# State-out weights of the S5 layer: imaginary parts on VectorE beside the gates, 25 of 32 pieces there instead of 19

## The chip, the core and the metric

The kernel runs on one core of a Trainium2 chip. The metric is device microseconds of one launch; lower is better. Engine names below: PE is TensorE, DVE is VectorE, ACT is ScalarE, POOL is GpSimd, SP is SyncE, which here only issues DMAs.

## The reference, cut to what matters

Two residual layers over 512 latent and 256 context tokens of width 1024. Layer 0 is multi-head latent attention with 16 heads and a SiLU gate of width 2048. Layer 1 is a bidirectional S5 state-space layer: 128 channel groups, each with 64 complex states in each direction.

```python
q_dn, kv_dn, k_rope, gate = split(h @ w_in)        # layer 0: the gate is 2048 wide = 16 tiles of 128
y = (softmax(q k^T) v * silu(gate)) @ w_out

lam_bar = exp(lam * dt)                            # layer 1, per direction, complex
xs[t]   = lam_bar * xs[t-1] + b_bar * u[t]
y[t]    = real(sum over states of xs[t] * cmat)    # two directions are summed
```

The kernel takes 8 tokens at a time as a block, so it needs, for each group, the complex products of `cmat` with the powers 0 to 7 of `lam_bar`: the state-out weights. They don't depend on the tokens. They are made in 32 pieces of 4 groups each.

## The kernel before, in words

The program goes through stages in order of time: modulation and first projections (to about 104 us), the 16 gate tiles of layer 0 (to 305 us), attention (from 331 to 757 us), layer 0's output projection, and then layer 1 (from about 890 us to the end). While layer 0 runs, the weights of layer 1's state space are prepared beside it: first the parameters (`s5_params`, on DVE and POOL, until 133 us), then the 32 pieces of state-out weights (`s5_chunk`, lines 335 to 373), then 32 pieces of state-in weights (`win_load` to `win_early`, lines 379 to 409) on POOL.

A piece of `s5_chunk` does this. SP loads `cb` (L339, two buffers), the `cmat` and `bmat` of four groups. POOL makes the real part `wr = cr*pr - ci*pi` (L351 to L353) and the imaginary part `wi = cr*pi + ci*pr` (L354 to L356) in the tile `wo`, with the scratch `wt1` of one buffer, then `b1`, `b2` (L361, L363) and two additions into `bk` (L367). `bks` are two tiles in turn, so the additions of a piece wait for the PE products of the piece two before. What comes after a piece is put off by one piece (`late`): `s5_lags` (lines 313 to 333) stores `wo` on SP's queue to `wod`, lets PE multiply `bk` with `wo` (L320, L323; below these are the lag products), has ACT and DVE copy the result to `ks` (L326, L327), and stores it on SP's queue with eight DMAs to `kd` (L330, L331). After every fourth piece SP copies `kd` to `toed` with eight DMAs (L311, `s5_lay`).

19 pieces (`S5IN`) run in the gate stage and 13 in attention. In the gate stage `tables(n)` is called behind each gate tile `m`; it emits one piece, or two at `m` = 3, 7, 11 and 15, and none at `m` = 0. The gate loop's other work: `gate(m)` takes 48 matmuls (L81, L82, L83) with a weight tile that ACT and DVE have split (L65), `mod_more` loads a part of the second layer's modulation weights on ACT's queue into one of two buffers `pair` and multiplies it (L103), `s5_coefs` runs at `m` = 4 (L296, L299), and the first head's query preparation at `m` = 11 to 13. PSUM tiles of the stage come from one pool of six buffers (`mm`). In attention a piece is emitted at every 1.6th of 80 units (a head's quarter of queries each, and a fifth unit for context); from unit `LAST` on, `win_early` is called in two of three units.

Each engine runs its own instructions in order. The order between engines' instructions is written down once, by a scheduler that works before the launch, so the place of an instruction in its queue is fixed, and an instruction that waits holds up all behind it on its engine.

Of the kernel before, what the change touches and what calls it, by code (L numbers as in the profile page):

```python
# [13 lines left out]
ALU = mybir.AluOpType  # L14
# [17 lines left out]
def hybrid_mla_s5(ctx, tc, I, O):  # L32
# [5 lines left out]
    pe, dve, act, pool, sp = nc.tensor, nc.vector, nc.scalar, nc.gpsimd, nc.sync  # L38
# [107 lines left out]
    G, Gd = [], {}  # L146


    GR, NCH, S5IN, WO = 128, 32, 19, [3]
    lamd = dram.tile([P, 2, GR], F32, name="lamd")  # L150
    pind = dram.tile([8, GR, 2, P], F32, name="pind")
    wod = [dram.tile([P, 4, 2, P], F32, name=f"wod{i}") for i in range(NCH)]
# [138 lines left out]
    def s5_coefs(cps, mm, tile):  # L291

        for k, cp in enumerate(cps):
            o = mm(256).rearrange("p (r x) -> p r x", r=2)
            for r in range(2):
                pe.transpose(o[:, r, :], cp[:, r, :], ident)  # L296
            st = tile()[:, :2 * P].rearrange("p (r x) -> p r x", r=2)
            act.copy(st[:, 0, :], o[:, 0, :])
            act.mul(st[:, 1, :], o[:, 1, :], -1.0)  # L299
            act.dma_start(out=pind[7 - k, :, :, 0:64], in_=st[:, :, 0:64])  # L300
            act.dma_start(out=pind[k, :, :, 64:128], in_=st[:, :, 64:128])
# [3 lines left out]
    def s5_lay():  # L305

        while whole:
            k = whole.pop()
            src = kd[k].rearrange("g c x -> c g x")
            for i in range(8):  # L310
                sp.dma_start(out=toed[k][16 * i:16 * i + 16], in_=src[:, :, 16 * (7 - i):16 * (7 - i) + P])  # L311

    def s5_lags(work, mm, c, wo, bk, dcol, eyek):

        sp.dma_start(out=wod[c], in_=wo)
        s5_lay()
        o = mm(P)
        for r in range(2):
            for q in range(4):
                pe.matmul(o[32 * q:32 * q + 32, :], bk[:, q, r, 0:32], wo[:, q, r, :], start=(r == 0), stop=False)  # L320
        for r in range(2):
            for q in range(4):
                pe.matmul(o[32 * q:32 * q + 32, 0:16], bk[:, q, r, 16:48], wo[:, q, r, 112:128],  # L323
                          start=False, stop=(r == 1))
        ks = work.tile([P, P], F32, name="ks", bufs=2)
        act.copy(ks[:, 16:P], o[:, 16:P])  # L326
        dve.scalar_tensor_tensor(ks[:, 0:16], eyek, dcol[:, c:c + 1], o[:, 0:16], op0=ALU.mult, op1=ALU.add)  # L327
        for q in range(4):
            g = 4 * (c % 4) + q
            sp.dma_start(out=kd[c // 4][g, :, 112:240], in_=ks[32 * q:32 * q + 16, :])  # L330
            sp.dma_start(out=kd[c // 4][g, :, 0:112], in_=ks[32 * q + 16:32 * q + 32, 0:112])  # L331
        if c % 4 == 3:
            whole.append(c // 4)

    def s5_chunk(work, mm, c, pw, cci, bks, dcol, eyek, end):

        def load(c):
            cbs[c] = work.tile([P, 4, 2, 32], F32, name="cb", bufs=2)
            sp.dma_start(out=cbs[c], in_=I["CB"][:, 4 * c:4 * c + 4])  # L339
        gs = slice(4 * c, 4 * c + 4)  # L340
        if c not in cbs:
            load(c)
        if c < end:
            load(c + 1)
        cb = cbs.pop(c)
        wo = work.tile([P, 4, 2, P], F32, name="wo", bufs=WO[0])
        t = work.tile([P, 4, 8, 16], F32, name="wt1", bufs=1)
        cr, ci = (cb[:, :, r, 0:16].unsqueeze(2).broadcast_to([P, 4, 8, 16]) for r in range(2))
        pr, pi = (pw[:, r, :, gs].rearrange("p j g -> p g j").unsqueeze(3).broadcast_to([P, 4, 8, 16]) for r in range(2))
        wr, wi = (wo[:, :, r, :].rearrange("p g (j c) -> p g j c", c=16) for r in range(2))  # L350
        pool.tensor_tensor(wr, cr, pr, op=ALU.mult)  # L351
        pool.tensor_tensor(t, ci, pi, op=ALU.mult)  # L352
        pool.tensor_tensor(wr, wr, t, op=ALU.subtract)  # L353
        pool.tensor_tensor(wi, cr, pi, op=ALU.mult)  # L354
        pool.tensor_tensor(t, ci, pr, op=ALU.mult)  # L355
        pool.tensor_tensor(wi, wi, t, op=ALU.add)  # L356

        b1 = work.tile([P, 4, 2, 16], F32, name="b1", bufs=1)
        b2 = work.tile([P, 4, 2, 16], F32, name="b2", bufs=1)
        bb = cb[:, :, :, 16:32]  # L360
        pool.tensor_tensor(b1, bb, cci[:, 0:2, gs].rearrange("p r g -> p g r").unsqueeze(3).broadcast_to([P, 4, 2, 16]),  # L361
                           op=ALU.mult)
        pool.tensor_tensor(b2, bb[:, :, ::-1, :], cci[:, 2, gs].unsqueeze(2).unsqueeze(3).broadcast_to([P, 4, 2, 16]),  # L363
                           op=ALU.mult)
        bk = bks[c % 2]
        for d, rows in enumerate((lo_, up_)):
            pool.tensor_tensor(bk[rows, :, :, 16 * d:16 * d + 16], b1[rows], b2[rows], op=ALU.add)  # L367
        late.append(lambda: s5_lags(work, mm, c, wo, bk, dcol, eyek))
        while len(late) > (c < end):
            late.pop(0)()  # L370
        if c == end:
            s5_lay()
# [38 lines left out]
    with ExitStack() as ctx_:  # L411
# [14 lines left out]
        def chunk(work, mm, c, end):  # L426
            s5_chunk(work, mm, c, pw, cci, bks, dcol, eyek, end)
# [103 lines left out]
        with mkpool(name="in_h", bufs=KC) as hp, mkpool(name="in_w", bufs=3) as wp, \  # L531
# [3 lines left out]
            def mm(n=512):  # L535
                return ps.tile([P, 512], F32, name="mm")[:, :n]
# [151 lines left out]
            def spill():  # L688
                while spills:
                    m = spills.pop()  # L690
                    Gd[m] = dram.tile([P, T], F32, name=f"gd0{m}")
                    act.dma_start(out=Gd[m], in_=G[m])

            def gate(m):
                w = wg.pop(0)
                G.append(gv.tile([P, T], F32, name="G") if m >= HEADS - KEPT else gsp.tile([P, T], F32, name="Gs"))
                gate_w()
                for a, b in LC:
                    o = mm(b - a)
                    proj_mm([o], w, range(KC), [(a, b)])  # L700
                    yield 1
                    act.activation(G[m][:, a:b], o, AF.Tanh, scale=0.5)
                    spill()
                    dve.scalar_tensor_tensor(G[m][:, a:b], G[m][:, a:b], 1.0, o, op0=ALU.add, op1=ALU.mult)
                if m < HEADS - KEPT:
                    spills.append(m)
# [40 lines left out]
            def mod_more():  # L747

                n = next(done)
                ends.get(n - 3, lambda: None)()  # L750
                if len(ready) == 2 or n > 24 and ready:
                    ready.pop(0)()
                for load, step in itertools.islice(steps, 1):
                    load()
                    ready.append(step)
            todo = iter(range(S5IN))

            def tables(n):
                for c in itertools.islice(todo, n):
                    chunk(s5in, mm, c, S5IN - 1)  # L760
            prep0 = dict(zip(range(11, HEADS), prep(0)))
            for m in range(HEADS):
                for _ in gate0 if m == 0 else gate(m):
                    mod_more()
                if m == 4:
                    s5_coefs(cps, mm, t512)
                for fn in prep0.pop(m, ()):
                    fn()
                tables((m > 0) + (m % 4 == 3))
            spill()  # L770
            sces.close()
        gv2 = gvs.enter_context(mkpool(name="gv2", bufs=HEADS - KEPT, side="right"))
# [226 lines left out]
    def res_load(tt, n):  # L999

        c = slice(512 * n, 512 * n + 512)
        if (n, tt // 4) not in gates0:
            g = gates0[n, tt // 4] = xp.tile([P, 512], F32, name="g", bufs=2)
            sp.dma_start(out=g, in_=gtrow[0][tt // 4:tt // 4 + 1, c].broadcast_to([P, 512]))
        x = xp.tile([P, 512], F32, name="x")
        sp.dma_start(out=x, in_=I["xp"][tt * P:(tt + 1) * P, c])
        return x, gates0[n, tt // 4]
# [4 lines left out]
    for h in range(HEADS):  # L1012
# [4 lines left out]
        if h < 9:  # L1017
            if 2 <= h < 8:
                tt = h - 2
                x, g = res_load(tt, 0)  # L1020
# [197 lines left out]
    for t in range(18):  # L1218
# [9 lines left out]
        m = t - 2  # L1228
# [90 lines left out]
    def glu_mm():  # L1319
        m, k, h = GLU_ORDER.pop(0)  # L1320
        wh, wl = wnext()
        if h == 0:
            if m % 4 in (1, 2):
                acc[m, k] = bank()
            elif k:
                t = two(m % 4 == 0)
                acc[m, 1], acc[m, 0] = t[:, 0], t[:, 1]
        for j in range(8):
            c = slice(j * P, (j + 1) * P)
            mm3(acc[m, k], wh[:, c], wl[:, c], *V[8 * h + j], (h, j) == (0, 0), (h, j) == (1, 7))  # L1330
        return m, k, h
# [33 lines left out]
    while GLU_ORDER:  # L1365
        m, k, h = glu_mm()
        if (k, h) == (0, 1):
            g = work.tile([P, TL], F32, name="g")
            sp.dma_start(out=g, in_=gd[m])
            t = work.tile([P, TL], F32, name="t2")  # L1370
# [10 lines left out]
    with mkpool(name="f_s", bufs=1, side="right") as work:  # L1381
# [34 lines left out]
        for tt in range(4):  # L1416
# [5 lines left out]
            for n in range(2):  # L1422
                c = slice(512 * n, 512 * n + 512)
# [106 lines left out]
```

## Time and profile before

| what | us |
|---|---|
| median of 3 runs | 1726.29 (1719.12 to 1726.81) |
| the profiled execution | 1721.6 |
| its span | 1719.5 |
| PE busy in the span | 1558.3 (91%) |
| DVE, ACT, POOL busy | 966.9, 728.7, 652.0 |
| POOL's last work in the attention stage | 749 |

PE is the engine with the most work, and from 757 us on it has little idle time. The stages in which other engines decide lie before that. Marks on the time line that are used below: the lag products of the first piece start at 136.15 us, gate tile 3 starts at 137 us, the last matmul of gate tile 15 starts at 304.93 us, and attention's first score matmul (L803) starts at 331.26 us.

### The profile page before, as it was taken

The page shows a single profiled execution, that of the slowest core. Times are in us where ns is not written, and L with a number is a line of the kernel's source. Part 1 is how long each engine was busy: PE and PEld are TensorE (multiplying, and loading weights), DVE is VectorE, ACT ScalarE, POOL GpSimd, SP SyncE. Part 2 cuts the span into 40 slices and gives each one's busy share as a digit, 9 for nine tenths or more (in the row PEclk, how much of TensorE's full clock was granted, in tenths as well). Part 3 has the DMA queues.
Part 4 walks back from the last instruction along what each step waited for, and adds up shares of the span by engine and source line. Part 5 has one row for each costly group of instructions (what it writes and reads, how often), then busy time and mean ns, then how long its engine had stood idle before and what let it go on. Part 6 is the DMA issues. An engine that isn't in the chain of part 4 may idle for free.

```text
span 1719.5 us, 26866 instructions
## 1 busy us (share of the span) xinstructions
PE 1558.3 (91%) x9870; PEld 1301.2 (76%) x9870; DVE 966.9 (56%) x2502; ACT 728.7 (42%) x1253; POOL 652.0 (38%) x682
## 2 busy tenths in 40 slices
PE   7867979499889999799999999999679999999997
PEld 4645857388778888688879999888568888888876
DVE  6541233177667887683372688899853333323347
ACT  2421222166446666563235666766562222222220
POOL 2999958859679989940021000000000000000022
PEclk9978999699999999999999999999889999999999
DMA  9266774443456666644327766398443333333432
GB/s 344 67 205 210 241 242 141 150 144 116 139 170 209 208 196 193 204 158 139 105 83 236 225 220 233 117 367 291 155 156 115 110 112 104 116 104 109 145 139 74
DMA packets 156459, 291.89 MB, mean 170 GB/s; under 512 B 55004, under 2 KB 86280, under 8 KB 155304
## 3 DMA queue, kind: packets, MB, share of 16 engines
q1 hardware_dynamic: 104112, 234.99, 40.0%
q10 hardware_dynamic: 52104, 55.03, 10.7%
q8 instruction: 78, 1.28, 0.3%
q14 instruction: 53, 0.43, 0.1%
q0 software_dynamic: 112, 0.16, 0.0%
HBM read 229.54 MB, written 68.70 MB: 173 GB/s over the span
## 4 chain that ended last, share of the span: by engine, by line
PE 59%; POOL 12%; DMA 10%; DVE 9%; ACT 4%; issue 3%; SPq 1%; ACTq 0%; POOLq 0%; DVEq 0%
PE mm L81 16%; PE mm L83 16%; PE mm L82 16%; PE mm L1157 3%; PE tr L842 2%; DMA wraw<-in_wout_dram 2%; DMA ext<-pind 2%; PE mm L1291 1%; DMA cb<-in_CB_dram 1%; POOL wo L356 1%; DMA toed<-kd 1%; POOL wo L354 1%; POOL wo L353 1%; POOL wt L355 1%; POOL wt L352 1%
## 5 line engine op out<-in xcount | busy, mean ns | idle before, releaser
L65 DVE TENSOR_TENSOR wlo<-wraw,whi 128x1024 fp32r<-128x1024 f32 (+1 forms) x155 | 179.1, 1157 | 327.7 <-ACT whi L65 324.4
L65 ACT CAST whi<-wraw 128x1024 fp32r<-128x1024 f32 (+1 forms) x155 | 149.3, 965 | 406.3 <-PE mm L82 270.9
L1394 POOL TENSOR_TENSOR x<-x,row_g 128x1024 f32<-128x1024 f32 x4 | 9.6, 2402 | 767.6 <-DMA x<-x1d 728.7
L81 PE MATMUL mm<-st,whi 128*128 128x512 f32 x512 | 204.1, 399 | 5.5 <-ACT st L76 5.4
L83 PE MATMUL mm<-st,wlo 128*128 128x512 f32 x512 | 202.7, 396 | 0.0
L82 PE MATMUL mm<-st,whi 128*128 128x512 f32 x512 | 201.2, 393 | 0.8 <-DVE st L77 0.8
L81 PE MATMUL mm<-h,whi 128*128 128x512 f32 (+1 forms) x384 | 139.4, 364 | 0.2 <-DVE bnmv L934 0.2
L82 PE MATMUL mm<-h,whi 128*128 128x512 f32 (+1 forms) x384 | 137.4, 358 | 0.6 <-DVE h L1094 0.6
L83 PE MATMUL mm<-h,wlo 128*128 128x512 f32 (+1 forms) x384 | 137.0, 357 | 0.0
L81 PEld LDWEIGHTS mm<-st,whi 128*128 128x128 f32 x512 | 97.5, 190 | 27.0 <-ACT st L76 6.6
L81 PE MATMUL mm<-hh,whi 128*128 128x512 f32 (+1 forms) x320 | 109.6, 355 | 7.3 <-ACT wmod L299 5.4
L82 PEld LDWEIGHTS mm<-st,whi 128*128 128x128 f32 x512 | 97.3, 190 | 23.4 <-DVE st L77 1.6
L83 PEld LDWEIGHTS mm<-st,wlo 128*128 128x128 f32 x512 | 97.3, 190 | 22.6
L83 PE MATMUL mm<-hh,wlo 128*128 128x512 f32 (+1 forms) x320 | 108.4, 343 | 1.8 <-DVE wlo L65 1.8
L82 PE MATMUL mm<-hl,whi 128*128 128x512 f32 (+1 forms) x320 | 109.4, 344 | 0.0
L818 ACT ACTIVATE p<-sc,mx 128x768 f32<-128x768 f32 (+1 forms) x96 | 73.5, 766 | 45.6 <-DVE mx L817 36.7
L65 DVE TENSOR_TENSOR ptl<-tr,pth 128x384 fp32r<-128x384 f32 (+1 forms) x160 | 78.7, 522 | 17.9 <-ACT pth L65 17.2
L65 ACT CAST pth<-tr 128x384 fp32r<-128x384 f32 (+1 forms) x160 | 68.1, 462 | 37.9 <-PE tr L842 31.6
L817 DVE TENSOR_REDUCE mx<-sc 128x1 f32<-128x768 f32 (+1 forms) x96 | 73.6, 770 | 18.4 <-PE sc L807 17.3
L81 PEld LDWEIGHTS mm<-h,whi 128*128 128x128 f32 x384 | 73.2, 191 | 12.1 <-issue 0.7
L82 PEld LDWEIGHTS mm<-h,whi 128*128 128x128 f32 x384 | 73.3, 191 | 11.0 <-DVE h L1094 1.1
L83 PEld LDWEIGHTS mm<-h,wlo 128*128 128x128 f32 x384 | 73.1, 191 | 10.4
(376 smaller groups left out, 4178.9 us busy)
## 6 DMA issues: line engine op xcount, KB each, us to landing
wraw<-in_wglu_dram SPq DMA_DIRECT2D x64, 512.0 KB
wraw<-in_win_dram SPq DMA_DIRECT2D x36, 512.0 KB
wod<-wo SPq DMA_DIRECT2D x32, 512.0 KB
pw<-in_Bc_dram SPq DMA_DIRECT2D x32, 512.0 KB
pt<-wid SPq DMA_DIRECT2D x32, 512.0 KB
wo<-wod SPq DMA_DIRECT2D x32, 512.0 KB
pair<-in_w_mod_dram ACTq DMA_DIRECT2D x16, 768.0 KB
wo<-pind SPq DMA_DIRECT2D x21, 512.0 KB
```

The lines of the kernel that those rows point to most:

```text
L65: return act.copy(hi, src).ins, (eng or dve).tensor_tensor(lo, src, f(hi), op=ALU.subtract).ins
L81: pe.matmul(ps, lh, rh, start=first, stop=False)
L82: pe.matmul(ps, lh, rl, start=False, stop=False)
L83: pe.matmul(ps, ll, rh, start=False, stop=last)
L352: pool.tensor_tensor(t, ci, pi, op=ALU.mult)
L353: pool.tensor_tensor(wr, wr, t, op=ALU.subtract)
L354: pool.tensor_tensor(wi, cr, pi, op=ALU.mult)
L355: pool.tensor_tensor(t, ci, pr, op=ALU.mult)
L817: dve.reduce_max(mx[:, 1:2], s, axis=AX.X, negate=True)
L818: act.activation(p[:, a:b], s, AF.Exp, bias=mx[:, 1:2], scale=1.0, accum_out=mx[:, 2:3])
L842: pe.transpose(tp[:, n, :], p[:, j * P:(j + 1) * P], ident)
L1157: pe.matmul(o[:, r, 96 * q:96 * (q + 1)], wi[:, q, r, :], us[m][:, 4 * (c % 2) + q, :], start=True, stop=True)
```

## The change

`S5IN` goes from 19 to 25, so 25 pieces are emitted beside the gates and 7 in attention; `LAST`, the attention unit from which `win_early` is called, goes with it from 20 to 11 by the line `LAST = 8 * (NCH - S5IN) // 5`. For the first 25 pieces the three operations of the imaginary part are issued on DVE instead of POOL, and their scratch is a PSUM tile of the gate stage's pool `mm` instead of `wt1`. `tables` emits two pieces behind each gate tile from `m` = 3 on, and none before.

```diff
-    GR, NCH, S5IN, WO = 128, 32, 19, [3]
+    GR, NCH, S5IN, WO = 128, 32, 25, [3]
...
         pool.tensor_tensor(wr, cr, pr, op=ALU.mult)
         pool.tensor_tensor(t, ci, pi, op=ALU.mult)
         pool.tensor_tensor(wr, wr, t, op=ALU.subtract)
-        pool.tensor_tensor(wi, cr, pi, op=ALU.mult)
-        pool.tensor_tensor(t, ci, pr, op=ALU.mult)
-        pool.tensor_tensor(wi, wi, t, op=ALU.add)
+
+        eng, t = (dve, mm(512).rearrange("p (g j c) -> p g j c", j=8, c=16)) if c < S5IN else (pool, t)
+        eng.tensor_tensor(wi, cr, pi, op=ALU.mult)
+        eng.tensor_tensor(t, ci, pr, op=ALU.mult)
+        eng.tensor_tensor(wi, wi, t, op=ALU.add)
...
-                tables((m > 0) + (m % 4 == 3))
+                tables(2 if m > 2 else 0)
```

Lines behind the edit move by two: L354 to L356 become L356 to L358, and L367 becomes L369.

On PE, in the queue of the kernel before, around the end of gate tile 2 (the last rows of it, then modulation products, then the lag products of the first piece, then gate tile 3, whose rows are again `hh`, 128x512):

```order
L81 MATMUL mm<-hh,whi 128x256
L82 MATMUL mm<-hl,whi 128x256
L83 MATMUL mm<-hh,wlo 128x256
L103 MATMUL modps<-pair,sT 2x384 x32
L320 MATMUL mm<-wo,ext 32x128 x8
L323 MATMUL mm<-wo,ext 32x16 x8
L81 MATMUL mm<-hh,whi 128x512
```

In the kernel after the change, gate tile 3 follows gate tile 2 directly; this is the end of its first half, the start of its second, with two modulation products inside:

```order
L83 MATMUL mm<-hh,wlo 128x512
L103 MATMUL modps<-pair,sT 2x384 x4
L81 MATMUL mm<-hh,whi 128x512
L82 MATMUL mm<-hl,whi 128x512
L83 MATMUL mm<-hh,wlo 128x512
L81 MATMUL mm<-hh,whi 128x256
L82 MATMUL mm<-hl,whi 128x256
L103 MATMUL modps<-pair,sT 2x384 x4
L83 MATMUL mm<-hh,wlo 128x256
```

and this its end, with three more modulation products (x12 is three times four), the first lag products, and gate tile 4:

```order
L82 MATMUL mm<-hl,whi 128x256
L83 MATMUL mm<-hh,wlo 128x256
L103 MATMUL modps<-pair,sT 2x384 x12
L320 MATMUL mm<-wo,ext 32x128 x8
L323 MATMUL mm<-wo,ext 32x16 x8
L81 MATMUL mm<-hh,whi 128x512
```

Gate tile 3 has moved ahead of the first lag products and of most of the modulation products that stood in front of it; three modulation products have moved behind the first lag products.

On DVE, in the kernel before, around one gate tile in the middle of the stage (`Gs` is a gate's last operation, `wlo` the split of a gate's weights, `ks` that of a lag product):

```order
L327 SCALAR_TENSOR_TENSOR ks<-eyek,dcol,mm 128x16
L704 SCALAR_TENSOR_TENSOR Gs<-Gs,mm 128x512
L65 TENSOR_TENSOR wlo<-wraw,whi 128x1024
L704 SCALAR_TENSOR_TENSOR Gs<-Gs,mm 128x256
L327 SCALAR_TENSOR_TENSOR ks<-eyek,dcol,mm 128x16
```

and in the kernel after the change:

```order
L65 TENSOR_TENSOR wlo<-wraw,whi 128x1024
L706 SCALAR_TENSOR_TENSOR Gs<-Gs,mm 128x256
L356 TENSOR_TENSOR wo<-cb,pw 128x4x128
L327 SCALAR_TENSOR_TENSOR ks<-eyek,dcol,mm 128x16
L924 TENSOR_TENSOR aff<-modc_1590,lnc 128x16
L925 TENSOR_TENSOR aff<-modc_1590,lnc 128x16
L327 SCALAR_TENSOR_TENSOR ks<-eyek,dcol,mm 128x16
L357 TENSOR_TENSOR mm<-cb,pw 128x512
L926 TENSOR_TENSOR aff<-aff,modc_1590 128x16
L358 TENSOR_TENSOR wo<-wo,mm 128x4x128
L356 TENSOR_TENSOR wo<-cb,pw 128x4x128
L357 TENSOR_TENSOR mm<-cb,pw 128x512
```

The operations of the imaginary part (L356 to L358) now stand between the gate's and the lag products' operations, and some `ks` stand behind an L356 of a later piece, which waits for that piece's `cb`.

## Rows read from the trace of the kernel before

**Rows 1.** Stages, 137 to 305 and 305 to 331 us: busy time, clock, DMA.

```profile
core 0: us, PE busy (x) PEld busy (x) DVE busy (x) ACT busy (x) POOL busy (x), PEclk, DMA share, GB/s
137.00:305.00 168.00, 147.91 (x1309) 119.76 (x1298) 48.88 (x92) 36.54 (x86) 140.57 (x160) 0.94 0.64 202
305.00:331.00 26.00, 3.52 (x98) 2.38 (x97) 1.70 (x5) 3.20 (x7) 25.60 (x31) 0.58 0.40 121
```

**Rows 2.** What PE waited for, 296 to 345 us: total, times, longest.

```profile
PE mm L320 <- POOL wo L356: 12.4, 2, 7.8
PE mm L320 <- POOL wo L353: 9.7, 1, 9.7
```

**Rows 3.** POOL by line, 113 to 337 us: busy us, mean ns, idle before.

```profile
L356 POOL TENSOR_TENSOR wo<-wo,wt 128x512 f32<-128x512 f32 x21 | 27.7, 1323 | 0.9
L353 POOL TENSOR_TENSOR wo<-wo,wt 128x512 f32<-128x512 f32 x21 | 27.7, 1317 | 0.6
L354 POOL TENSOR_TENSOR wo<-cb,pw 128x512 f32<-128x512 f32 x21 | 25.6, 1217 | 0.0
L352 POOL TENSOR_TENSOR wt<-cb,pw 128x512 f32<-128x512 f32 x22 | 24.3, 1105 | 0.9
L355 POOL TENSOR_TENSOR wt<-cb,pw 128x512 f32<-128x512 f32 x21 | 23.2, 1105 | 0.9
L351 POOL TENSOR_TENSOR wo<-cb,pw 128x512 f32<-128x512 f32 x21 | 23.2, 1105 | 23.2 <-DMA cb<-in_CB_dram 15.0 <-issue 7.9
L367 POOL TENSOR_TENSOR ext<-b,b 64x128 f32<-64x128 f32 x42 | 22.9, 545 | 1.6
L361 POOL TENSOR_TENSOR b<-cb,ext 128x128 f32<-128x128 f32 x21 | 10.9, 517 | 0.0
L363 POOL TENSOR_TENSOR b<-cb,ext 128x128 f32<-128x128 f32 x21 | 8.8, 420 | 0.0
```

**Rows 4.** What PE waited for, 104 to 137 us.

```profile
PE modps L103 <- DMA pair<-in_w_mod_dram: 17.8, 8, 5.0
```

**Rows 5.** POOL in order of time: start us, us; the first piece's additions.

```profile
135.11 0.98 POOL L367 TENSOR_TENSOR ext<-b,b 64x128 f32<-64x128 f32 x2
```

**Rows 6.** PE in order of time: the lag products ahead of gate tile 4.

```profile
147.41 0.65 PE L320 MATMUL mm<-wo,ext 128*32 128x128 f32 x16 [0.20 <-POOL ext L367]
```

**Rows 7.** SP's queue in order of time, 281 to 306 us.

```profile
281.54 0.42 SPq L331 DMA_DIRECT2D kd<-ks  x1
282.00 0.42 SPq L330 DMA_DIRECT2D kd<-ks  x1
...
282.98 0.37 SPq L339 DMA_DIRECT2D cb<-in_CB_dram  x1
283.46 0.37 SPq L315 DMA_DIRECT2D wod<-wo  x1
...
303.62 2.60 SPq L311 DMA_DIRECT2D toed<-kd  x4
```

**Rows 8.** What SP's queue waited for, 137 to 331 us.

```profile
SPq L339 <- POOL wt L355: 28.2, 7, 7.0
```

**Rows 9.** DVE by line and form, 137 to 331 us: busy us, mean ns.

```profile
L65 DVE TENSOR_TENSOR wlo<-wraw,whi 128x1024 fp32r<-128x1024 f32 x10 | 15.7, 1572 | 29.3 <-ACT whi L65 27.4 <-DMA wmod<-in_bgt_dram 1.8
```

**Rows 10.** The same view, 1300 to 1600 us, where POOL does nothing.

```profile
L65 DVE TENSOR_TENSOR wlo<-wraw,whi 128x1024 fp32r<-128x1024 f32 x55 | 67.4, 1226 | 170.8 <-ACT whi L65 169.9
```

**Rows 11.** Score matmuls of L803, two a unit: busy (count) in two stretches.

```profile
431.00:531.00 100.00, 12.72 (x36) 7.21 (x36) 0.95 0.54 165
545.00:643.00 98.00, 13.63 (x40) 7.53 (x40) 1.00 0.61 201
```

**Rows 12.** PE by line and form, 340 to 470 us, with 13 pieces.

```profile
L320 PE MATMUL mm<-wo,ext 128*32 128x128 f32 x208 | 8.7, 279 | 1.4 <-POOL wo L356 1.4
...
L323 PE MATMUL mm<-wo,ext 128*32 128x16 f32 x208 | 3.8, 182 | 0.0
```

**Rows 13.** What PE waited for, 530 to 740 us.

```profile
PE sc L803 <- ACT pair L65: 6.8, 2, 5.9
```

## The prediction, made before the changed kernel ran

> **What bounds the kernel now.** I read the busy time by stages first, then what PE waited for where it idles, then the engine it waited for, line by line, and last the queues. The change touches the gate stage and attention, so only what happens before 757 us can move. From 137 us, where gate tile 3 starts, to 305 us, where gate tile 15 ends, PE is busy for 147.9 of 168 us. Then it is nearly idle, 3.5 of 26 us, until attention's first score matmul at 331.3 us, and the granted clock is 0.58 there, while POOL is busy for 25.6 of these 26 us [rows 1]. PE waits there for lag products of the last pieces, whose `wo` POOL has not made: 12.4 and 9.7 us [rows 2]. So the stage ends by POOL. Its price per piece is the sum of means: L351 1.105, L352 1.105, L353 1.317, L354 1.217, L355 1.105, L356 1.323, L361 0.517, L363 0.420 and twice L367 at 0.545, together 9.20 us, and there are 23.2 us of idle time ahead of L351, 15.0 of them put down to `cb` [rows 3]. Nineteen pieces at 9.20 and the idle time make 198 us, which is what lies between the end of the parameters (133 us) and 331. SP in turn waits for POOL: 28.2 us before it may load the next `cb` [rows 8]. DVE has work for 48.9 of 168 us [rows 1], and DMA stands at a share of 0.64.
>
> **The imaginary part on DVE, what POOL loses.** L354, L355 and L356 leave POOL: 3.645 us a piece, so 5.55 us stay. What DVE pays for them no row shows for this shape, so from the nearest: a subtraction of twice as many elements, with both inputs in SBUF, takes 1226 ns while POOL does nothing [rows 10] and 1572 ns in the gate stage [rows 9]. So 0.61 us is the price of one in peace, and 0.35 us what POOL's company adds. The two products read two SBUF tiles, 0.96 each; the addition reads PSUM for one of its inputs, 0.61. That is 2.5 us a piece and 63 us for 25, beside DVE's 49 in a stage of some 170: DVE has the room. POOL pays for the company too: its mean for L354 is 0.11 over that of L351, the same shape [rows 3]. A product on DVE can hold it up for nothing at least and for the whole 0.61 at most, so 0 to 1.2 us a piece. I take 0.7, nearer to the upper end because DVE's own loss is more than half of a price in peace: 6.25 us a piece.
>
> The Trainium skill says more on this ("SBUF — State Buffer", section "Who interferes with whom"): a DVE instruction with two SBUF inputs contends with a GpSimd instruction that reads SBUF, and whoever comes second is blocked for the whole of the other. The 346 ns between [rows 9] and [rows 10] agree with it. By that rule POOL would pay at the upper end, 6.75 us a piece, and what this gives is the second rival below.
>
> **The head of the stage.** Before, PE waits 17.8 us in 104 to 137 us for eight loads of modulation weights [rows 4], and gate tile 3 stands behind all of them and behind the first lag products. Those need POOL's additions of piece 0, which start at 135.1 us [rows 5]. Gate tile 4 starts behind the lag products of 147.41 + 0.65 [rows 6], at 148 us. After, gate tile 3 stands ahead of most of these waits and three of the modulation products stand behind the lag products. The tile takes some 9 us, less than the 17.8 us of waits that it now fills. The additions come earlier by what stands ahead of them in POOL's order now, three L354, two L355 and two L356, 8.5 us by [rows 3], less some 2 to 3 us for DVE's company: 129 us. So gate tile 4 can start at 131 us. At the other end gate tile 3 is not hidden, because the loads come too late, and gate tile 4 starts at 140. I take 134, 14 us earlier, nearer to the first because the loads' order is the same and only fewer of them are needed.
>
> **The stage from gate tile 4 on: three counts.** Twelve gate tiles, the lag products of pieces 1 to 24, and pieces 3 to 24 lie behind it.
> PE: the 147.9 us of [rows 1] less the 11 us before 148; ten more lag products at 12.5 us for 13 [rows 12], 0.96 each, 9.6 us; three more modulation products, taken at the same price, 3 us. That is 150 us. It had 20.1 us of gaps in its 168 us [rows 1], and I keep them: loads of modulation weights that now stand close together make new ones, the waits for POOL become fewer. 170 us, to 304.
> POOL: 22 pieces at 6.25 us are 137.5 us; its idle time of 23.2 us for 21 pieces [rows 3] is kept in proportion, 24 us. From 131 us that ends at 293.
> SP: 0.46 us from one `kd` store to the next and 0.48 from `cb` to `wod`; four `toed` copies take 2.60 us [rows 7]. A piece costs 8 x 0.46 + 2 x 0.48 + a quarter of 5.2, so 5.9 us. Before POOL's 9.2 this was hidden; beside 6.25 it is not by much. The `cb` of piece 24 stands behind the stores of piece 21: 22 x 5.9 = 131 us from 131, and 0 to 28 us of waits as in [rows 8]; with 15, 277 us, and 10 us more for the last piece itself.
> So PE is late next, at 304 us, with POOL and SP close behind. The queues hold each other up in turn: the next `cb` stands behind `kd` stores on SP, these behind `ks` on DVE, some of these behind an L356 that waits for a `cb`. For that I add 3 us: attention starts at 307 instead of 331.3, 24 us earlier. The bounds are 298 (PE without most of its gaps) and 318 (gate tile 4 at 140, 8 us of lock-step more).
> The scratch in PSUM takes one more of six buffers for a piece; a gate tile takes two and a piece two now, so a buffer comes round only after about a whole gate tile. I cost that at nothing; if a tile has to wait for DVE's addition, it is the third rival's price.
>
> **Attention.** Six pieces fewer: 6 x 0.96 = 5.8 us of PE's time. In 431 to 531 us, with the last pieces and the start of the state-in weights, 36 score matmuls fit in 100 us, and in 545 to 643 us 40 in 98 [rows 11], so that stretch loses more than its pieces cost; that change of work on POOL moves to an earlier unit and I leave it as it is. Bounds: 0, if PE waits for others in the freed time, and 12, if the change-over costs less where it falls now. I take 6. State-in weights start some nine units earlier; POOL's end in attention (749 us) is off the path then, and before it was just ahead of attention's end.
>
> **Sum.** 1721.6 - 24 - 6 = 1691.6 us, against the profiled execution. That lies 4.7 us under the median of the runs shown, and the three spread over 7.7 us; I put half of that on top: 1694 us. The likeliest case's own range is 1677 to 1708.
>
> **Rivals.**
> 1. More than that: POOL and SP keep up, and PE loses most of its gaps. From 131 us, 150 us of PE work and 5 of gaps end at 286, 45 us earlier; with 6 us from attention and the 5.9 us wait for `pair` near its end [rows 13], if it is DMA traffic of the state-in weights that makes it, 1665 us. For it: the counts of POOL and SP leave room. Against: PE's gaps before were not all POOL's.
> 2. Hardly any gain, POOL stays the bound: 6.75 us a piece, and the idle time for `cb` twice as long because the loads must come in 6.75 instead of 9.2 us: 22 x 6.75 + 46 = 195 us from 131, attention at 329 with its last lag products, 1721.6 - 2 - 6 = 1713 us. For it: [rows 9], and SP's 5.9 us a piece. Against: SP waited for POOL [rows 8], not the other way, for most of the time.
> 3. Slower: DVE's queue carries the wait for `cb`. In the new order the splits of the gate's weights and the gate's own operations stand behind L356, which waits for `cb`, so a late load stops PE's next gate tile as well. Price: the four waits for `cb` make 15.0 us [rows 3], 3.75 us each; one at each of 12 pairs of pieces adds 45 us to 304: 349 us, 18 us later, less 6: 1734 us. It decides from 2.75 us a pair on, 33 us in all, where attention would start at 337 and its 6 us be used up. For it: the DMA share rises with six more pieces in less time. Against: only four waits in 21 pieces before, and a load stands about two pieces ahead.
>
> **How the numbers follow.** 0.5% of this kernel is 8.6 us, about what a measurement can tell from no change: faster means under 1717.7. The forecast has 0.60, rival 1 0.16, rival 2 0.14, rival 3 0.10. Faster: 0.60 + 0.16 + 0.09 of rival 2 = 0.85. Within 0.5%: 0.05 of rival 2 and 0.02 of rival 3, 0.07. Slower: 0.08 of rival 3. The range goes from 1670 to 1720 us: the third rival and the far end of the first are left out.
>
> **What would show it.** The idle time of PE before attention's first score matmul gone or under 5 us, and that matmul near 307 us; gate tile 4's first matmul near 134; POOL at 5.6 to 6.8 us a piece; DVE at 2.5 us a piece with its two products near 0.96 and more than its addition; SP hardly idle in 200 to 300 us. Rival 2 would show as lag products that still wait for POOL, rival 3 as L356 on DVE waiting for `cb` and matmuls of a gate tile waiting for `wlo`. The forecast is wrong if attention starts after 320 us, or if attention itself takes longer than its 426 us.

## The result, and the profile after

The change made the kernel slower by 1%: 1739.55 us (median of 5 runs, 1738.73 to 1750.23) against 1724.23 us (5 runs, 1719.12 to 1726.81), a ratio of 1.0106 with a 95% interval of 1.008 to 1.0132. The forecast was 1694 us. The profiled execution after is the 1750.23 us one, 10.7 us above its median, so the marks below are up to that much late.

| mark | before | forecast | after |
|---|---|---|---|
| gate tile 4's first matmul | 148 | 134 | 135.6 |
| attention's first score matmul | 331.3 | 307 | 368.4 |
| attention's length | 425.5 | 419.5 | 417.3 |
| from attention's end to the span's end | 962.7 | the same | 962.7 |
| the span | 1719.5 | | 1748.4 |

All of the loss lies between gate tile 4 and attention. Stages of after: the first two lines are the stretches of [rows 1], then the rest of the gate stage, and the whole of it from gate tile 4 on (columns as there).

```profile
137.00:305.00 168.00, 114.16 (x1089) 88.77 (x1088) 74.75 (x119) 28.73 (x72) 95.32 (x111) 0.79 0.62 193
305.00:331.00 26.00, 21.61 (x170) 18.82 (x169) 12.22 (x17) 5.48 (x11) 18.05 (x21) 0.87 0.55 169
331.00:368.00 37.00, 24.01 (x277) 20.71 (x279) 19.64 (x30) 6.81 (x16) 28.16 (x33) 0.87 0.39 120
135.80:368.00 232.20, 160.97 (x1534) 129.25 (x1538) 106.84 (x167) 41.20 (x99) 141.53 (x163) 0.81 0.58 179
```

In the first 168 us PE did 114.2 us of work where it did 147.9 before, and POOL 95.3 instead of 140.6. Over the whole 232 us no engine is full: PE is busy for 161.0, POOL for 141.5, DVE for 106.8. The mean granted clock is 0.81, between the levels of 1.2 and 2.4 GHz, where it was 0.94 in the first line of [rows 1], and the DMA share of 0.58 is lower than before.

What POOL does per line, 113 to 372 us, answers to [rows 3]:

```profile
L351 POOL TENSOR_TENSOR wo<-cb,pw 128x512 f32<-128x512 f32 x25 | 36.7, 1470 | 67.3 <-DMA cb<-in_CB_dram 62.3 <-DVE ks L327 4.7
L352 POOL TENSOR_TENSOR wt<-cb,pw 128x512 f32<-128x512 f32 x25 | 34.5, 1379 | 0.4
L353 POOL TENSOR_TENSOR wo<-wo,wt 128x512 f32<-128x512 f32 x25 | 33.0, 1320 | 0.1
L369 POOL TENSOR_TENSOR ext<-b,b 64x128 f32<-64x128 f32 x50 | 27.3, 546 | 13.9 <-PE mm L320 11.9
L363 POOL TENSOR_TENSOR b<-cb,ext 128x128 f32<-128x128 f32 x24 | 14.2, 593 | 0.2
L365 POOL TENSOR_TENSOR b<-cb,ext 128x128 f32<-128x128 f32 x24 | 12.6, 523 | 0.0
```

and DVE's three new groups, 125 to 368 us:

```profile
L357 DVE TENSOR_TENSOR mm<-cb,pw 128x512 f32<-128x512 f32 x23 | 27.9, 1212 | 11.8 <-ACT wmod L299 11.8
L356 DVE TENSOR_TENSOR wo<-cb,pw 128x512 f32<-128x512 f32 x23 | 19.8, 860 | 56.7 <-DMA cb<-in_CB_dram 41.0 <-issue 6.6 <-DMA toed<-kd 5.9
L358 DVE TENSOR_TENSOR wo<-wo,mm 128x512 f32<-128x512 f32 x23 | 15.5, 681 | 0.3
```

The prices are near the forecast: POOL 1.470 + 1.379 + 1.320 + 2 x 0.546 + 0.593 + 0.523 = 6.38 us a piece (6.25), DVE 0.86 + 1.21 + 0.68 = 2.75 us (2.5). What is new stands behind the last bar: 62.3 us in which POOL waits for `cb`, against 15.0 before, and 41.0 us in which DVE does. What PE waits for, 125 to 368 us (total, times, longest), answers to [rows 2, 4]:

```profile
PE mm L320 <- POOL ext L369: 39.7, 7, 11.2
PE modps L103 <- DMA pair<-in_w_mod_dram: 30.7, 9, 9.7
PE mm L320 <- DVE wo L358: 4.0, 3, 2.3
PE mm L81 <- DVE ks L327: 2.5, 1, 2.5
```

PE waits for the lag products' inputs, and these for `cb`. Why is `cb` late? SP's queue in order of time, ahead of the last load of the stage (columns as in [rows 7]):

```profile
345.22 5.09 SPq L311 DMA_DIRECT2D toed<-kd  x8
350.36 0.60 SPq L331 DMA_DIRECT2D kd<-ks  x1
351.00 0.42 SPq L330 DMA_DIRECT2D kd<-ks  x1
...
357.01 0.42 SPq L331 DMA_DIRECT2D kd<-ks  x1
357.53 0.37 SPq L339 DMA_DIRECT2D cb<-in_CB_dram  x1
```

and the chain that ends with attention's first score matmul (start us, us, what), over the same time:

```profile
343.25 1.96 DMA kd<-ks
345.22 0.54 SPq L311
...
357.01 0.42 SPq L331
357.53 3.07 DMA cb<-in_CB_dram
360.67 0.09 issue
360.77 1.58 POOL wo L351
...
366.73 0.46 POOL ext L369
367.24 1.08 PE mm L320 x16
368.32 0.19 PE mm L323 x16
368.50 0.73 PE sc L805
```

For 12.3 us the chain is nothing but SP issuing eight `toed` copies and fifteen `kd` stores, one by one. Only then is the load issued that POOL has waited for; it takes 3.07 us, then POOL's piece and the lag products follow. The longest of POOL's waits is of the same kind. The load for piece 9 takes the buffer of piece 7, whose last reader (L365) ends at 190.74 us; SP issues the load at 217.66, behind sixteen `kd` stores, eight `toed` copies and a `wod` store:

```profile
190.34 0.40 POOL L365 TENSOR_TENSOR b<-cb,ext 128x128 f32<-128x128 f32 x1
217.66 0.37 SPq L339 DMA_DIRECT2D cb<-in_CB_dram  x1
220.12 1.52 POOL L351 TENSOR_TENSOR wo<-cb,pw 128x512 f32<-128x512 f32 x1 [13.98 <-DMA cb<-in_CB_dram]
```

In the six longest of POOL's waits for `cb`, 51 of the 62.3 us, the buffer had been free for 4 to 27 us when SP came to the load. So the two buffers of `cb` were not the limit there; a third was not tried.

The stores that stand ahead of a `cb` follow lag products of an earlier piece, and these that piece's own `cb`. So the work goes round in a loop: `cb`, POOL and DVE, lag products, `ks`, `kd` stores, the next `cb`.

From 130 us to attention SP's queue spends 134 us issuing 276 DMAs (101 us and 215 before; each a sum over the timeline). So SP itself is a little over half busy, and yet it is in the loop. What it waits for in the rest, 125 to 368 us:

```profile
SPq L339 <- DVE mm L357: 18.8, 2, 12.8
SPq L339 <- POOL b L365: 13.9, 4, 9.0
SPq L330 <- DVE ks L327: 4.7, 3, 2.5
```

The first two lines are loads that do wait for their buffer. The wait for `ks` itself is small. Some 50 us more are waits for other transfers to land, 10.6 of them for `pair`, a load on ACT's queue; why a store or copy waits for those is not shown.

### The profile page after: what moved, and what is told of

The parts are those of the page before. It is cut to its first block, busy times and chain, and to the rows that moved or that the text cites. A ratio compares the mean times of both kernels' runs of the same rounds, so it can differ in the third digit from the quotient of the medians.

```text
span 1748.4 us, 26921 instructions
## 1 busy us (share of the span) xinstructions
PE 1568.5 (90%) x9870; PEld 1309.6 (75%) x9870; DVE 1028.5 (59%) x2577; ACT 730.1 (42%) x1253; POOL 586.0 (34%) x607
## 4 chain that ended last, share of the span: by engine, by line
PE 53%; DMA 12%; DVE 10%; POOL 6%; ACT 4%; issue 3%; SPq 3%; ACTq 0%; POOLq 0%; DVEq 0%
PE mm L81 14%; PE mm L83 14%; PE mm L82 14%; PE mm L1159 3%; DMA wraw<-in_win_dram 2%; DMA wraw<-in_wout_dram 2%; DMA kd<-ks 2%; DMA cb<-in_CB_dram 1%; PE tr L844 1%; DMA wod<-wo 1%; SPq L311 1%; SPq L331 1%; DVE wlo L65 1%; PE sc L808 1%; SPq L330 1%
## 5 line engine op out<-in xcount | busy, mean ns | idle before, releaser
L65 DVE TENSOR_TENSOR wlo<-wraw,whi 128x1024 fp32r<-128x1024 f32 (+1 forms) x155 | 177.9, 1149 | 316.9 <-ACT whi L65 315.8
L81 PE MATMUL mm<-hh,whi 128*128 128x512 f32 (+1 forms) x320 | 113.8, 368 | 4.9 <-DVE ks L327 2.5
L83 PE MATMUL mm<-hh,wlo 128*128 128x512 f32 (+1 forms) x320 | 112.5, 355 | 1.8 <-DVE wlo L65 1.8
L82 PE MATMUL mm<-hl,whi 128*128 128x512 f32 (+1 forms) x320 | 113.4, 357 | 0.0
L65 DVE TENSOR_TENSOR ptl<-tr,pth 128x384 fp32r<-128x384 f32 (+1 forms) x160 | 78.7, 523 | 25.7 <-ACT pth L65 25.1
```

The lines of the kernel that those rows point to most:

```text
L65: return act.copy(hi, src).ins, (eng or dve).tensor_tensor(lo, src, f(hi), op=ALU.subtract).ins
L81: pe.matmul(ps, lh, rh, start=first, stop=False)
L82: pe.matmul(ps, lh, rl, start=False, stop=False)
L83: pe.matmul(ps, ll, rh, start=False, stop=last)
```

## The experiments

Theory A: the loop through SP's in-order queue sets the stage; what is issued ahead of a `cb` load is paid in full. Theory B: POOL and DVE slow each other, or DVE's new work holds up the gates. Theory C: too many bytes in too little time, so DMA's bandwidth sets it. All kernels compute the whole output. A scheduler orders each of them anew, so an edit also moves some instructions that it does not touch (e6 and e9 show how much that can be). Attention's first score matmul is the mark that is compared; ratios are against the kernel before on the same chip. The profiled execution of each run gives the marks.

**e1: the `cb` load leaves SP's queue** (otherwise the changed kernel).

```diff
-            sp.dma_start(out=cbs[c], in_=I["CB"][:, 4 * c:4 * c + 4])
+            (pool if c < S5IN else sp).dma_start(out=cbs[c], in_=I["CB"][:, 4 * c:4 * c + 4])
```

> The changed kernel with one edit: the loads of cb for the 25 pieces of the gate stage are issued from POOL's queue instead of SP's, where each stood behind the kd stores and toed copies of earlier pieces. Theory A (the gate stage is a loop through SP's queue: a piece waits for its cb, whose issue waits behind the kd stores of the pieces before, which wait for the lag products of the piece): the 62 us that POOL waits for cb shrink to under 20, attention's first score matmul comes at 310 to 335 us instead of 368, the time is 1695 to 1715 us. Theory B (DVE and POOL hold each other up, on the port or in DVE's queue): no more than 8 us from the changed kernel's 1740. Theory C (too many bytes in too little time, DMA-bound): the same as B.

1719.92 us (10 runs), ratio 0.9983 (0.996 to 1.0006); attention starts at 340.0. The load now waits for no store, and 28 us of the stage are gone: the direction is theory A's, but attention's start and the time both missed its ranges by about 5 us. POOL's waits for `cb` (130 to 340 us) are replaced by shorter ones for SP's stores, which free `wo`, and for DVE's product, which frees a buffer of `cb` for the next load:

```profile
POOL wo L351 <- DMA wod<-wo: 20.3, 7, 7.6
POOL cb L339 <- DVE mm L357: 11.8, 4, 6.4
```

**e2: one `kd` store a piece instead of eight**; the layout of `kd` changes with it, and the copies to `toed` become 15 instead of 8 for four pieces.

```diff
-        for q in range(4):
-            g = 4 * (c % 4) + q
-            sp.dma_start(out=kd[c // 4][g, :, 112:240], in_=ks[32 * q:32 * q + 16, :])
-            sp.dma_start(out=kd[c // 4][g, :, 0:112], in_=ks[32 * q + 16:32 * q + 32, 0:112])
+        sp.dma_start(out=kd[c // 4][4 * (c % 4):4 * (c % 4) + 4].rearrange("q z i x -> (q z i) x"), in_=ks)
```

> The changed kernel with another layout of kd in memory, so that a piece is stored by one DMA instead of eight, and every fourth piece is copied to toed by 15 DMAs instead of eight: SP issues 3.9 us a piece instead of 5.9, the bytes stay. Theory A: attention's first score matmul at 325 to 350 us, the time 1705 to 1727 us. Theory B: within 8 us of the changed kernel's 1740. Theory C: the same as B, since no byte goes away.

1701.33 us (4 runs), ratio 0.9876 (0.9828 to 0.9924); attention starts at 327.6, 41 us earlier, as theory A had it, and the time is 4 us better than its range. SP issues 146 DMAs in 79 us. POOL's wait (125 to 330 us):

```profile
POOL wo L351 <- DMA cb<-in_CB_dram: 25.1, 7, 7.7
```

**e7: the opposite dose, sixteen `kd` stores of half the size.**

```diff
-            sp.dma_start(out=kd[c // 4][g, :, 112:240], in_=ks[32 * q:32 * q + 16, :])
-            sp.dma_start(out=kd[c // 4][g, :, 0:112], in_=ks[32 * q + 16:32 * q + 32, 0:112])
+            for i in (0, 8):
+                sp.dma_start(out=kd[c // 4][g, i:i + 8, 112:240], in_=ks[32 * q + i:32 * q + i + 8, :])
+                sp.dma_start(out=kd[c // 4][g, i:i + 8, 0:112], in_=ks[32 * q + 16 + i:32 * q + 24 + i, 0:112])
```

> The changed kernel with the kd stores of a piece cut into 16 DMAs of half the size instead of eight, the bytes and the packets the same: SP issues 9.6 us a piece instead of 5.9, 3.7 us more, for 25 pieces 92 us. Theory A: most of it is seen in the gate stage, attention's first score matmul at 420 to 460 us, the time 1785 to 1830 us. If POOL, DVE or the bytes set the stage: within 10 us of 1740.

1769.08 us (4 runs), ratio 1.0252 (1.0225 to 1.0279); attention starts at 391.7. The direction is theory A's, the size is less than I had expected: the issue of a store of half the size is shorter, 0.34 us from one to the next instead of 0.46, so SP's issue time rose to 158 us and not by the double of the stores. SP's queue, and POOL's wait (125 to 392 us):

```profile
342.49 0.29 SPq L332 DMA_DIRECT2D kd<-ks  x1
342.83 0.29 SPq L331 DMA_DIRECT2D kd<-ks  x1
343.17 0.29 SPq L332 DMA_DIRECT2D kd<-ks  x1
```

```profile
POOL wo L352 <- DMA cb<-in_CB_dram: 100.5, 20, 28.6
```

Bytes are the same in the changed kernel and here; 25.1, 62.3 and 100.5 us of waits for `cb` go with 1, 8 and 16 stores. The 24 us of issue time more than in the changed kernel come back, by the marks, as 23 us by which attention starts later. Theory A holds.

**e3: the imaginary part back on POOL, still 25 pieces.**

```diff
-        eng, t = (dve, mm(512).rearrange("p (g j c) -> p g j c", j=8, c=16)) if c < S5IN else (pool, t)
+        eng, t = (pool, t)
```

> The changed kernel with the imaginary parts back on POOL: 25 pieces beside the gates, two behind each gate tile from the fourth on, all on POOL. Theory A: the loop through SP stays and POOL has 9.2 us a piece in it instead of 6.4, so slower than the changed kernel: 1750 to 1780 us. Theory B: without DVE's part nothing holds POOL up, 1720 to 1740 us, faster than the changed kernel. Theory C: within 10 us of the changed kernel.

1747.31 us (4 runs), ratio 1.0147 (1.0106 to 1.0189); attention starts at 381.5. To take DVE's work away does not help, so theory B is not the cause of the loss. Theory A's 1750 to 1780 us was missed by 3 us, and the interval overlaps the changed kernel's, as theory C had it; against C speak e1 and e2, in which it expected no gain, and the DMA share in e5. POOL's wait for `cb` falls to 23.8 us (125 to 382 us), because POOL's own 25 pieces are the longer part again:

```profile
POOL wo L351 <- DMA cb<-in_CB_dram: 23.8, 8, 12.2
```

**e4: DVE's part alone, 19 pieces placed as before.**

```diff
-    GR, NCH, S5IN, WO = 128, 32, 25, [3]
+    GR, NCH, S5IN, WO = 128, 32, 19, [3]
...
-                tables(2 if m > 2 else 0)
+                tables((m > 0) + (m % 4 == 3))
```

> The imaginary parts on DVE as in the changed kernel, but 19 pieces beside the gates and one behind most gate tiles, as in the kernel before. Theory A: one piece to a gate tile leaves SP room (5.9 us in some 11), so POOL's shorter pieces are felt: attention starts at 300 to 325 us, 1695 to 1720 us. Theory B: no faster than the kernel before, 1724 to 1740 us. Theory C: like A, 1700 to 1720 us.

1720.06 us (10 runs), ratio 0.998 (0.9958 to 1.0001). The stage gains the 24 us that I had forecast for the whole change, attention starts at 307.2, but attention takes 441.2 us instead of 425.5. Not all of the gain need be DVE's part: POOL has two pieces fewer under way at that mark than before (see e6). With 19 pieces attention ends shortly behind POOL's last work there: 739.8 and 748.4 us here, 749.8 and 756.8 before, 725.5 and 733.4 in e8 below. After the change it ends 40 us behind it. So POOL's 13 pieces and state-in weights seem to end attention when only 19 pieces go ahead; that was read from the marks and not tested by an edit of its own, and e8 and e11, with 19 pieces as well, take 428.1 and 430.7 us. Beside e4 the six pieces cost 1.3% (1.0106 against 0.998, the intervals apart).

**e5: both relief edits, e1's and e2's, on the changed kernel.**

> The changed kernel with both edits of the first runs: cb loaded from POOL's queue in the gate stage, and a piece's kd stored by one DMA (15 instead of 8 toed copies every fourth piece). Theory A (the loop through SP's queue sets the gate stage): SP has the issue of kd, wod and toed left, 3.4 us a piece, and no cb stands behind it; attention's first score matmul at 305 to 325 us, the time 1680 to 1698 us. If what is left in the run with kd alone (attention at 327.6 us, 1701 us) is set by POOL or by DVE instead, it stays at 1698 to 1708 us.

1691.7 us (4 runs), ratio 0.9808 (0.9793 to 0.9823): faster than both kernels, and as theory A had it. Attention starts at 315.8. The same stretch as the first line above, then what PE waits for, 130 to 330 us:

```profile
137.00:305.00 168.00, 145.47 (x1443) 115.95 (x1442) 110.36 (x159) 37.88 (x92) 143.60 (x173) 0.92 0.75 236
```

```profile
PE mm L323 <- POOL ext L369: 13.6, 5, 3.4
PE mm L323 <- POOL wo L353: 7.0, 2, 3.7
PE modps L103 <- DMA pair<-in_w_mod_dram: 5.6, 3, 3.5
```

With SP relieved the waits for `ext` fall from 39.7 to 13.6 us, and those for the modulation weights from 30.7 to 5.6 us, though their loads are on ACT's queue and were not edited: they were a consequence too. The DMA share rises to 0.75, so DMA's bandwidth was not what held the stage.

**e6: the kernel before, with one `kd` store a piece.** This asks whether POOL hid SP's queue before, as I had written.

> The kernel before the change with the same store of kd in one DMA. Theory A: there POOL's 9.2 us a piece hid SP's 5.9, so little comes of it: 1712 to 1726 us, attention's first score matmul at 320 to 331 us. If the store is a gain by itself whatever the rest of the kernel (fewer waits on DMA queues everywhere), it brings as much as in the changed kernel, 38 us: below 1700 us.

1704.31 us (4 runs), ratio 0.9881 (0.9854 to 0.9909); attention starts at 311.8, not 331.3. I had expected little from it if POOL was the bound, and 38 us if the store is a gain by itself; it gained 20 us, between the two. POOL's idle time ahead of L351, 113 to 312 us, where [rows 3] have 23.2 us:

```profile
L351 POOL TENSOR_TENSOR wo<-cb,pw 128x512 f32<-128x512 f32 x20 | 23.4, 1172 | 12.9 <-DMA cb<-in_CB_dram 12.3 <-issue 0.2
```

The shorter idle time explains 10 of the 20 us. The other 10 are POOL's work: from 133 us to attention's start POOL is busy for 170.3 us before and for 160.6 in e6 (last column but three; the third line is e9, below).

```profile
133.00:331.30 198.30, 154.18 (x1427) 123.09 (x1423) 50.78 (x97) 41.62 (x97) 170.31 (x197) 0.89 0.61 193
133.00:311.80 178.80, 155.50 (x1431) 123.91 (x1423) 52.25 (x97) 42.37 (x97) 160.62 (x183) 0.90 0.67 210
133.00:327.90 194.90, 155.91 (x1426) 122.69 (x1423) 56.32 (x97) 42.00 (x97) 181.44 (x216) 0.89 0.63 195
```

Attention's first score matmul stands behind the lag products of 19 pieces in all three, but when it starts POOL has made `b1` and `b2` (L361, L363) of 21 pieces before and in e9, and of 19 in e6: there the scheduler put work on two of attention's pieces ahead of the last operations for the 19th. So SP's queue cost time before the change as well, some 10 us, and the order of POOL's work as much.

**e8: e4 with one `kd` store a piece.**

> Imaginary parts on DVE, 19 pieces beside the gates as before, and kd in one DMA. With 13 pieces left in attention, POOL ended its state-in weights 8 us before attention ended, in the kernel before (749.8 of 756.8 us) and with DVE's part and 19 pieces (739.9 of 748.4). Theory A with this: the gate stage gets shorter still, attention's first score matmul at 290 to 305 us, but attention takes 435 to 450 us because POOL's work in it sets its end: 1700 to 1715 us, not better than with 25 pieces (1701). If attention is not set by POOL, the gain of the gate stage is kept: 1685 to 1695 us.

1697.75 us (4 runs), ratio 0.9853 (0.9829 to 0.9878); attention starts at 305.3 and takes 428.1 us. The time lies between my two expectations, 1700 to 1715 us and 1685 to 1695. The store edit takes 13 us off e4's attention and little off its stage.

**e9 to e12: the change's two parts once SP is relieved.** All four have both edits of e5. e9 is the kernel before with them, e10 is e5 with the edit of e3, e11 is e5 with the edits of e4, and e12 has 22 pieces:

```diff
-    GR, NCH, S5IN, WO = 128, 32, 25, [3]
+    GR, NCH, S5IN, WO = 128, 32, 22, [3]
...
-                tables(2 if m > 2 else 0)
+                tables((m > 0) + (m % 2 == 1 and m > 1))
```

> The kernel before with both relief edits of e5 (one `kd` store a piece, `cb` loaded on POOL's queue). Main theory: with SP relieved POOL bounds this gate stage, 19 pieces at 9.2 us from 133 us, so the second edit adds next to nothing to the first: attention starts at 306 to 314, about 1698 to 1706 us, where e6 had 1704. Rival: SP's queue still costs as much as it did in the changed kernel, where the second edit was worth 10 us: attention under 304, 1690 to 1697 us.

> e5 with the imaginary part back on POOL, still 25 pieces in the gate stage. Main theory: once SP is out of the way the three operations on DVE are worth what the prediction counted, 9.2 against 6.4 us a piece on POOL: 25 pieces at 9.2 us from 133 us end at 363 us, attention starts at 355 to 370, about 1725 to 1745 us against e5's 1692. Rival, that moving them to DVE gains nothing even then because both engines are slowed by each other: attention within 10 us of e5's 316, 1690 to 1702 us.

> e5 with 19 pieces in the gate stage, placed as before the change. Main theory: the six pieces cost about as much beside the gates as in attention once SP is relieved; attention starts at 300 to 306 and takes 426 to 432 us, 1690 to 1699 us, within 0.4% of e5's 1692. Rival, that the move of six pieces is the whole of e5's gain: 1700 us or more. The other way, that the six pieces are still too many for the stage: under 1686 us.

> e5 with 22 pieces in the gate stage, two behind each odd gate tile from 3 on and one behind the others but the first. Halfway between e5 and e11: attention starts at 304 to 311 and takes 417 to 423 us, 1685 to 1693 us. If the stage is bounded by PE up to 22 pieces and by the loop through SP and POOL beyond, it is the fastest of the three, at 1685 to 1689 us; if the price of a piece is the same on both sides, all three lie within 4 us.

| kernel | imaginary part | pieces beside the gates | attention starts | its length | median us | ratio (95%) |
|---|---|---|---|---|---|---|
| e9 | POOL | 19 | 327.9 | 431.3 | 1723.18 (10 runs) | 0.9986 (0.9963 to 1.0009) |
| e10 | POOL | 25 | 382.2 | 410.3 | 1756.64 (4) | 1.0175 (1.0126 to 1.0224) |
| e11 | DVE | 19 | 300.2 | 430.7 | 1693.19 (4) | 0.9811 (0.9763 to 0.9859) |
| e12 | DVE | 22 | 305.3 | 418.3 | 1687.48 (4) | 0.9788 (0.9748 to 0.9828) |
| e5 | DVE | 25 | 315.8 | 413.8 | 1691.7 (4) | 0.9808 (0.9793 to 0.9823) |

e9 missed both expectations: the second edit does not add nothing, it takes back all that the first gave (e6: 0.9881). Its rows say why; POOL, 113 to 312 us:

```profile
L351 POOL TENSOR_TENSOR wo<-cb,pw 128x512 f32<-128x512 f32 x20 | 23.2, 1160 | 8.4 <-DMA cb<-in_CB_dram 6.6 <-DMA wod<-wo 1.3 <-issue 0.4
L339 POOL DMA_DIRECT2D cb<-in_CB_dram x17 | 9.8, 579 | 0.0
```

There POOL hardly waits: it is the bound, and each load that it issues itself takes 0.58 us of its time, 9.8 us here, of the 16 us by which attention starts later than in e6. By the three lines at e6 POOL has 20.8 us more work ahead of attention than in e6 and 4.7 us less idle time; the work that is not loads, some 11 us, is that on two of attention's pieces. So e9 does not show the price of the second edit by itself. The same edit helps where POOL has time to spare (e1, e5) and gave no gain where it has none (e9, e10).

e10 missed by its size too, by about that much: with 0.58 us on top of 9.2, 25 pieces end near 377 us, and attention started at 382.2, not at 355 to 370. Beside e5 it shows what DVE's part is worth once SP is out of the way: 66 us of the stage and about 65 us of the time. At 19 pieces it is 30 us of the time (e9 and e11). Both figures hold the order of POOL's work too: e9 and e10 have two pieces more under way at attention's start than e11 and e5. e11 and e12 came as the main expectation had them; which of e12's two finer cases holds can't be told. The number of pieces is then worth nothing that can be told: what e11 gains in the stage it pays in attention. e12 has the best median, but e5, e11 and e12 lie within 6 us and their intervals overlap.

## Why the prediction was wrong

**What bounds the kernel.** "So the stage ends by POOL" was half right. POOL's work was the longest, but one edit on SP's queue alone took 20 us off the stage (e6), 10 of them idle time of POOL. That 19 x 9.20 us and the idle time gave just 198 us was luck: three of the pieces were begun before 133 us, and work on two of attention's pieces stood ahead of the stage's end.

**The head of the stage** came out near: gate tile 4 started at 135.6 us (forecast 134), the first lag products at 134.4. But POOL's additions for them came at 133.4, not at 129; what fitted was the 3 us of allowance on top of 131. The modulation loads cost 8.0 us instead of 17.8 up to there.

**The prices of a piece** were right: 6.38 and 2.75 us (DVE's two products 0.86 and 1.21 instead of 0.96 each). The Trainium skill ("SBUF — State Buffer", section "Who interferes with whom") has a DVE instruction with two SBUF inputs and a GpSimd instruction that reads SBUF contend. The trace agrees that they do: L351, L352 and L353 (the subtraction) in e10, where DVE has no such products in the stage, 113 to 385 us:

```profile
L353 POOL TENSOR_TENSOR wo<-wo,wt 128x512 f32<-128x512 f32 x27 | 35.7, 1321 | 1.6
...
L352 POOL TENSOR_TENSOR wt<-cb,pw 128x512 f32<-128x512 f32 x27 | 30.0, 1110 | 0.6
L351 POOL TENSOR_TENSOR wo<-cb,pw 128x512 f32<-128x512 f32 x27 | 29.9, 1107 | 8.7 <-DMA cb<-in_CB_dram 5.1 <-DMA wod<-wo 2.0 <-issue 1.4
```

After the change the two products take 1.470 and 1.379 us; the subtraction takes the same. In the pairs that differ in DVE's products alone the size is smaller: 1.174 and 1.147 us in e3 against these, 1.107 and 1.110 in e10 against 1.311 and 1.310 in e5. What a whole block would have cost, 6.75 us a piece, was not reached.

**The three counts from gate tile 4 on: this is the step that failed.** I counted 150 us of PE work, 22 x 6.25 us of POOL and 22 x 5.9 us of SP, let each run beside the others, and took the latest. The work itself came out near that: PE 161.0 us at the lower clock, POOL 141.5 us. What failed is the idle time. I kept POOL's at 24 us "in proportion", and it was 232.2 - 141.5 = 90.7 us; I kept PE's at 20.1 us, and it was 71.2 us. SP's 5.9 us a piece had no place beside the others: the `cb` of a piece stands behind `kd` stores that follow an earlier piece's lag products, so SP's issue time, and the transfers that it waits for, come after PE's work and before POOL's, in one loop. SP's own count was right, 131 us against 134 measured; that it could run beside the others was wrong. The prediction named this order ("the next `cb` stands behind `kd` stores on SP, these behind `ks` on DVE, some of these behind an L356 that waits for a `cb`") and priced it at 3 us. The price was that of 232.2 against 170 us, some 60 us, of which e5 got back 53 by edits of nothing but DMAs that SP had issued.

**"Before POOL's 9.2 this was hidden"** was wrong already for the kernel before, by the 10 us of idle time that e6 took away. The waits of SP for POOL [rows 8] were taken as proof that SP had time to spare. In a loop, each member waits for the others by turns, and SP's waits for POOL and POOL's for `cb` stood in the same profile.

**The forecast's signs.** "SP hardly idle in 200 to 300 us" did not come: SP was busy for 134 of 238 us and still set the pace. PE's lag products did still wait for POOL, 39.7 us, the sign that I had given to rival 2; but POOL had been waiting for `cb` in its turn.

**The rivals.** Rival 3, slower by the wait for `cb` on DVE's queue, gave 1734 us and came nearest, and its sign was there: L356 waits for `cb` 11 times, 41.0 us. But its path was not: it had the gate tiles wait for `wlo`, and PE's longest wait of a gate matmul on DVE was 2.5 us. The lateness reached PE through POOL and the lag products. Its chance of 0.10 was too small: it was argued from four waits in 21 pieces, at POOL's old pace, which the change itself took away. Rival 2 had POOL's idle time twice as long, 46 us, where it was four times.

**Attention** came out near: 8.2 us shorter, forecast 6. That is in part luck: with the same seven pieces left it took 404.7 us in e2, 416.0 in e1 and 417.3 here. That POOL's end is then off the path was right as well, and e4 shows what that can be worth: with 19 pieces attention gives back 15.7 of 24 us there (5.2 us longer than before in e11).

## What to carry to other kernels

Before adding up engines side by side, look for a loop: a load that stands on an in-order queue behind stores which wait for what the load feeds. In such a loop issue times, transfers and work add up, a faster engine only waits longer, and a queue that is half idle can set the pace; take the load to a queue with time to spare, or make the stores ahead of it fewer. Moving a DMA's issue to a compute engine is paid in that engine's time, 0.58 us of POOL's for each load here: check that it is not the next bound. And when a scheduler orders the instructions anew, count what an engine has done at the mark that you compare, before the whole difference is put down to the edit.

## What was not expected of the hardware

- The issue of a DMA on SP's queue cost 0.46 us from one `kd` store to the next, 0.34 us when the store was halved (e7), and 0.64 us for a `toed` copy (eight in 5.09). On POOL's queue the issue of a `cb` load cost 0.58 us of POOL's time. The Trainium skill ("DMA: Bandwidth & Descriptors", section "Issuing engines are not separate DMA queues") has it that issuing from several engines saves only the time to initiate, which is usually small beside the DMA. One issue here agrees with that, 0.46 us beside a load's 3.07; what adds up is their number, and the 12.3 us of issues ahead of that load were four times its own time.
- The two products on DVE have the same inputs and shape, but L357, which writes to PSUM, took 1212 ns, and L356, which writes to SBUF, 860 ns. In e5 it was 1335 and 1115. POOL's products run beside both; whether the output's place or POOL's company makes the difference was not separated.
